# Query tiles loaded once to half of the partitions, and written to both halves by GpSimd

## The chip, the cores and the metric

The kernel runs on one core of a Trainium2 chip. The metric is the device time of one execution in microseconds. Times of before are three executions and one more under the profiler.

## What is computed

One layer of an encoder over 2048 tokens (a grid of 32 rows by 64 columns) of width 1024, in float32. Only the neighbourhood attention matters for the change; the rest is dense products around it.

```python
h = rms_norm(x, norm1_g[l])
proj = h @ w_in[l]
...
q = rms_norm(q, q_g) * jnp.asarray(hd ** -0.5, dtype=q.dtype)
k = rms_norm(k, k_g)
...
sc = jnp.einsum('bhqd,bhiqjd->bhqij', q_r, k_win).astype(jnp.float32)
sc = sc + bias[None]
p = jax.nn.softmax(sc.reshape(bsz, n_h, GRID_W, kh * WIN_COLS), axis=-1)
return jnp.einsum('bhqij,bhiqjd->bhqd', p, v_win)
...
merged = gates[..., :D_MODEL] * (y_a @ w_o_a[l]) + gates[..., D_MODEL:] * (y_b @ w_o_b[l])
x = x + merged @ w_out[l]
h2 = rms_norm(x, norm2_g[l])
x = x + jnp.square(jax.nn.relu(h2 @ w_ff1[l])) @ w_ff2[l]
```

Each query sees a window of 8 rows by 16 columns of keys; there are 8 heads of 64.

## The kernel before, in words

A float32 operand is split into a high part and a low rest (both float32r), so that three fast products replace one slow one. The stages follow one another: the projections and gates, the values and queries, the attention, the merge with the output projection, and twice the two products of the MLP. Intermediate results go through tensors in DRAM: `qs` holds the queries (64 dimensions by head of a pair, part, pair and token), `ks` the keys.

The attention goes through 16 units, 4 pairs of heads by 4 blocks of 8 grid rows. `unit` (L1152) plans the loads of one: for each of the two heads a key tile (`load_k`, L1162) and a query tile (`load_q`, L1173, and `order`, L1178), then value tiles and bias tiles. The key tile holds the keys' high parts in partitions 0 to 63 and their low rests in 64 to 127, 64 dimensions each. A product with it therefore wants the query's 64 dimensions twice, in both halves of the partitions. `load_q` gets them by two DMAs from the same place of `qs`, one to each half (L1176). `order` then makes the tile `q` from the loaded `qn` by four copies on GpSimd, one for each block of 16 columns, which reorder the tokens and round to float32r (L1181). A copy has 128 partitions and 256 elements in each.

`scores` (L1221) computes one column block: the product of q and keys on PE (L1234), on VectorE the bias and the maximum (L1248), on ScalarE the exponential (L1249), then the normalising multiply of one head on VectorE (L1256) and of the other on ScalarE (L1259). `turn` transposes the result on PE (L1279) and copies it out of PSUM (L1286, L1289); `products` multiplies it with the values (L1306). Between them stand fill products of the other branch (`branch_units`, L335), 32 in all, with inputs `y`, gates `g` and results `ma`.

The order of all instructions comes from a planner (`Plan`, L88). PE's steps are a list. Everything that prepares a step or follows one is a chain of stages, each with an engine, a cost in microseconds, the buffers that it takes and gives back, and a lead: so long before the first step that needs the chain it is issued at the latest. The planner walks along the steps with a clock for each engine, issues a stage earlier where the engine, its inputs and the buffers (51 in all) allow it, and may put a stage of ScalarE or VectorE off by a step. Nearly all transfers are issued on SP's queue. The cost of a stage only moves the planner's clocks, and so the order.

Of the kernel before, what the change touches and what calls it, by code (L numbers as in the profile page):

```python
# [24 lines left out]
HD = 64  # L25
# [249 lines left out]
class Block:  # L275
# [876 lines left out]
    def unit(self, pair, rb):  # L1152


        nc, plan = self.nc, self.plan
        r0, n, _ = ROWBLK[rb]
        rows = range(r0 // 2, (r0 + n + 1) // 2)
        ks, qs, vs = [], [], []
        for hd in range(2):
            e = {}  # L1160

            def load_k(e=e, hd=hd):  # L1162
                e[0] = self.take([n, GW], F32R, "kst")
                nc.sync.dma_start(
                    e[0][1].rearrange("p r c -> p (r c)").bitcast(F32),
                    self.ks[:, :, hd, pair, r0 * GW : (r0 + n) * GW].rearrange("l d t -> (l d) t"),
                )

            give = lambda e=e: self.give(e[0][0])
            ks.append((e, plan.chain([Stage("SP", 1.6, load_k, 1, 0, 12, 3.0)], tuple(self.k_done[t] for t in rows), hold=(1, give))))  # L1170
            e = {}

            def load_q(e=e, hd=hd):  # L1173
                e[1] = self.take([2, 512], F32, "qn")
                for dup in range(2):
                    nc.sync.dma_start(e[1][1][dup * HD : (dup + 1) * HD], self.qs[:, hd, :, pair, rb * 512 : (rb + 1) * 512])  # L1176

            def order(e=e):  # L1178
                e[0] = self.take([4, 2, P], F32R, "q")
                for cb in range(4):  # L1180
                    nc.gpsimd.tensor_copy(  # L1181
                        e[0][1][:, cb].rearrange("p l (r c) -> p (l r) c", c=16),
                        e[1][1].rearrange("p l (r f c) -> p f (l r) c", f=4, c=16)[:, cb],
                    )
                self.give(e[1][0])

            give = lambda e=e: self.give(e[0][0])
            qs.append((e, plan.chain([Stage("SP", 1.8, load_q, 1, 0, 16, 3.0), Stage("POOL", 3.0, order, 1, 1, 6, 0.3)], tuple(self.q_done[t] for t in range(4 * rb, 4 * rb + 4)), hold=(1, give))))
        for c2 in range(2):
            e = {}  # L1190

            def load_v(e=e, c2=c2):
                e[0] = self.take([2, 4, P], F32, "vw")
                for cb in range(2 * c2, 2 * c2 + 2):
                    w = COLBLK[cb][1]
                    per = P // w
                    f = n // per
                    v = e[0][1][:, cb % 2]
                    src = self.vs[cb][r0 : r0 + n, :, pair * P : (pair + 1) * P]
                    nc.sync.dma_start(v[: per * w, :f, :], src[: f * per].rearrange("(j r) k d -> (r k) j d", r=per))  # L1200
                    if n % per:
                        nc.sync.dma_start(v[: n % per * w, f, :], src[f * per :].rearrange("r k d -> (r k) d"))

            give = lambda e=e: self.give(e[0][0])
            vs.append((e, plan.chain([Stage("SP", 2.4, load_v, 1, 0, 10, 3.0)], tuple(self.v_done[t] for t in rows), hold=(1, give))))
        if rb != 2:
            kind = ROWBLK[rb][2]
            for ct in range(3):
                e = {}

                def load_b(e=e, ct=ct, kind=kind):
                    w = KIND_N[kind] * KIND_W[ct]
                    e[0] = self.take([2, w], F32, "bias")
                    src = self.tb[ct][kind][2 * pair : 2 * pair + 2].rearrange("h r c k -> (r c) h k")
                    nc.sync.dma_start(e[0][1], src)

                give = lambda e=e: self.give(e[0][0])
                self.bias[pair, ct, kind] = (e, plan.chain([Stage("SP", 1.6, load_b, 1, 0, 10, 3.0)], (self.bias_done,), hold=(1, give)))
        return ks, qs, vs

    def scores(self, pair, rb, cb, unit):  # L1221

        nc, plan = self.nc, self.plan
# [42 lines left out]
    def turn(self, rb, cb, p):  # L1266
# [25 lines left out]
        return e  # L1292

    def products(self, rb, cb, unit, pT, po, o):
        nc, plan = self.nc, self.plan
        n, w = ROWBLK[rb][1], COLBLK[cb][1]
# [121 lines left out]
    POOL, MM = 1.5, 0.2267  # L1418
# [556 lines left out]
```

## Time and profile before

| | |
|---|---|
| three executions | 2676.95, 2681.66, 2684.58 us (median 2681.66) |
| profiled execution | 2676.33 us, span 2674.6 us |
| busy in the span | PE 95%, DVE (VectorE) 68%, ACT (ScalarE) 45%, POOL (GpSimd) 45% |
| attention stage | 838 to 1117 us of the span |
| moved in the run | 569.14 MB, mean 213 GB/s |

The span is from the first to the last instruction; the profiled execution's own time holds 1.7 us more. An engine that is idle costs nothing unless the next work waits for it, so the rows on who waits for whom matter more than the busy shares.

### The profile page before, as it was taken

What the parts mean: (1) busy time and instruction counts of PE and PEld (TensorE: products, weight loads), DVE (VectorE), ACT (ScalarE), POOL (GpSimd) and SP (SyncE); (2) the same over time, 40 slices, a digit from 0 to 9 for tenths busy, and PEclk for the clock granted to TensorE, in tenths of its full rate; (3) what the DMA queues carried; (4) which work ended last, traced back from release to release, by engine and by line L of the source; (5) the groups of instructions that cost most, each with busy time, mean ns of one, the idle gap of its engine ahead of it and who ended that gap; (6) DMA issues with size and microseconds to landing.
All of it is one profiled execution on the core that took longest, in us unless ns stands there. A gap on an engine that the chain in (4) does not pass through costs nothing.

```text
span 2674.6 us, 34179 instructions
## 1 busy us (share of the span) xinstructions
PE 2533.7 (95%) x11832; PEld 2054.3 (77%) x11832; DVE 1809.7 (68%) x2492; ACT 1196.6 (45%) x1889; POOL 1206.0 (45%) x828
## 2 busy tenths in 40 slices
PE   7999999997898899899998999899999999989999
PEld 6777887875777677688887888787787888868777
DVE  5668657658677565563646555788878556688786
ACT  6556446555444555532343343543334434453331
POOL 3565554433341111142535676654344767655341
PEclk9999999998999999999999999999999999999999
DMA  6878768778679999987765443655446544465442
GB/s 202 268 242 269 226 234 285 210 223 274 175 199 270 305 325 308 335 295 244 260 228 179 152 146 142 235 173 171 138 135 216 197 149 151 146 220 192 150 146 98
DMA packets 409962, 569.14 MB, mean 213 GB/s; under 512 B 36606, under 2 KB 280382, under 8 KB 409790
## 3 DMA queue, kind: packets, MB, share of 16 engines
q1 hardware_dynamic: 405646, 566.96, 66.3%
q8 instruction: 93, 1.52, 0.2%
q10 hardware_dynamic: 4144, 0.02, 0.1%
q14 instruction: 79, 0.65, 0.1%
HBM read 363.89 MB, written 202.98 MB: 212 GB/s over the span
## 4 chain that ended last, share of the span: by engine, by line
PE 64%; DMA 11%; DVE 10%; issue 2%; SPq 2%; ACT 2%; POOL 0%; DVEq 0%; ACTq 0%; POOLq 0%
PE z L1555 26%; PE x L1555 13%; PE fg L335 12%; PE y L1555 7%; DVE r_lo L1436 2%; DVE x_r L1523 2%; DVE o L1886 2%; PE z L725 2%; PE pv L1306 1%; PE s L1234 1%; DMA x_r<-wf 1%; DMA vw<-vs 1%; DMA x_r<-xf 1%; PE x L725 1%; PE pTp L1279 1%
## 5 line engine op out<-in xcount | busy, mean ns | idle before, releaser
L1555 PE MATMUL z<-x_t,t_hi 128*128 128x512 f32 x1184 | 369.0, 393 | 23.6 <-DVE o L1886 15.1
L1478 POOL TENSOR_TENSOR w_s<-w_r 128x512 f32<-128x512 f32 (+3 forms) x87 | 153.1, 1759 | 431.5 <-PE z L1555 243.4
L1436 DVE TENSOR_TENSOR r_lo<-w_r,r_hi 128x1024 fp32r<-128x1024 f32 (+3 forms) x174 | 272.2, 1565 | 64.7 <-ACT r_hi L1432 60.3
L1555 PEld LDWEIGHTS z<-x_t,t_hi 128*128 128x128 f32 x1184 | 219.9, 188 | 81.6 <-ACT r_hi L1432 14.2
L1555 PE MATMUL z<-x_t,t_lo 128*128 128x512 f32 x592 | 231.3, 391 | 0.0
L1432 ACT CAST r_hi<-w_r 128x1024 fp32r<-128x1024 f32 (+3 forms) x174 | 171.3, 985 | 102.8 <-PE z L1555 75.6
L1555 PE MATMUL x<-x_r,t_hl 128*128 128x512 f32 x888 | 215.8, 391 | 0.2 <-DVE x_r L1523 0.2
L1555 PEld LDWEIGHTS x<-x_r,t_hl 128*128 128x128 f32 x888 | 167.0, 188 | 36.1 <-DVE x_r L1523 0.7
L1555 PE MATMUL z<-x_t,r_hi 128*128 128x512 f32 x592 | 184.2, 392 | 7.9 <-DVE o L1886 7.6
L1555 PE MATMUL z<-x_r,r_hi 128*128 128x512 f32 x592 | 186.2, 396 | 2.2 <-DVE x_r L1523 2.2
L1555 PE MATMUL y<-x_r,r_hi 128*128 128x512 f32 x592 | 182.5, 389 | 0.0
L1555 PE MATMUL x<-x_r,r_hi 128*128 128x512 f32 x592 | 182.3, 389 | 0.0
L335 PE MATMUL fg<-y,w_hi 128*128 128x512 f32 x512 | 163.2, 400 | 12.3 <-DMA y<-ya 8.0
L1523 DVE TENSOR_TENSOR x_r<-x_r,x_r 128x1024 fp32r<-128x1024 f32 x104 | 154.5, 1498 | 26.3 <-ACT x_r L1519 26.1
L1181 POOL CAST q<-qn 128x256 fp32r<-128x256 f32 x128 | 48.2, 419 | 254.3 <-DMA qn<-qs 162.1
L1479 POOL TENSOR_TENSOR w_r<-w_r,w_r 128x512 f32<-128x512 f32 (+3 forms) x87 | 152.5, 1752 | 12.4 <-issue 2.8
L335 PE MATMUL fg<-mg,w_hi 128*128 128x512 f32 x512 | 157.8, 389 | 0.0
L1484 POOL TENSOR_TENSOR w_s<-w_r 128x512 f32<-128x512 f32 (+3 forms) x87 | 154.6, 1777 | 4.2
L1519 ACT CAST x_r<-x_r 128x1024 fp32r<-128x1024 f32 x104 | 108.4, 1052 | 93.6 <-PE x L1555 29.3
L1519 ACT CAST x_t<-x_t 128x1024 fp32r<-128x1024 f32 (+1 forms) x104 | 85.0, 835 | 130.1 <-PE z L1555 110.1
L1485 POOL TENSOR_TENSOR w_s<-w_r,w_s 128x512 f32<-128x512 f32 (+3 forms) x87 | 118.4, 1360 | 46.4 <-DVE r_lo L1436 21.9
L1436 DVE TENSOR_TENSOR t_lo<-w_s,t_hi 128x1024 fp32r<-128x1024 f32 (+3 forms) x87 | 137.8, 1586 | 1.7 <-ACT t_hi L1432 1.7
(255 smaller groups left out, 6070.0 us busy)
## 6 DMA issues: line engine op xcount, KB each, us to landing
w_r<-in_w_ff_dram SPq DMA_DIRECT2D x116, 512.0 KB
x_r<-af SPq DMA_DIRECT2D x64, 512.0 KB
w_r<-in_w_in_dram SPq DMA_DIRECT2D x34, 512.0 KB
gt<-fe SPq DMA_DIRECT2D x32, 512.0 KB
x_r<-xf SPq DMA_DIRECT2D x32, 512.0 KB
qn<-qs SPq DMA_DIRECT2D x64, 256.0 KB
g<-gt SPq DMA_DIRECT2D x64, 256.0 KB
x<-x SPq DMA_DIRECT2D x32, 512.0 KB
```

Of the source, the lines that this page charges most:

```text
L335: self.nc.tensor.matmul(out, w[p], x[q], start=(i == 0 and j == 0), stop=(i == n - 1 and j == 2))
L725: nc.tensor.matmul(out, a[u], b[v], start=(p in (1, 5, 2) and k == 0 and j == 0), stop=(k == 3 and j == 2), skip_group_check=p in (6, 3, 7 ...
L1432: nc.scalar.copy(e[name + "_"][1][0], e[name][1])
L1436: nc.vector.tensor_tensor(lo, e[name][1], hi.bitcast(F32), ALU.subtract)
L1478: nc.gpsimd.tensor_tensor(s23[:, :, 1], r1[:, :, 0], r1[:, :, 1], ALU.subtract)
L1479: nc.gpsimd.tensor_tensor(r1[:, :, 1], r1[:, :, 1], r2[:, :, 1], ALU.add)
L1484: nc.gpsimd.tensor_tensor(s23[:, :, 0], r1[:, :, 1], r1[:, :, 0], ALU.subtract)
L1485: nc.gpsimd.tensor_tensor(e["t4"][1], r2[:, :, 0], s23[:, :, 0], ALU.subtract)
L1519: nc.scalar.copy(hi, lo.bitcast(F32))
L1523: nc.vector.tensor_tensor(lo, lo.bitcast(F32), hi.bitcast(F32), ALU.subtract)
L1555: nc.tensor.matmul(out, a[u], b[v], start=(p in (1, 5, 2) and k == 0 and j == 0), stop=(k == n - 1 and j == 2), skip_group_check=p in (6, ...
L1886: nc.vector.tensor_tensor(v, bank, v, ALU.add)
```

## The change

One DMA loads the query tile to partitions 0 to 63. For each column block two copies of 64 partitions on GpSimd take the place of one of 128: the first writes the lower half, the second reads the lower half of `qn` and writes the upper half of `q`. The planner's costs of the two stages become 0.9 (from 1.8) and 3.6 (from 3.0).

```diff
             def load_q(e=e, hd=hd):
                 e[1] = self.take([2, 512], F32, "qn")
-                for dup in range(2):
-                    nc.sync.dma_start(e[1][1][dup * HD : (dup + 1) * HD], self.qs[:, hd, :, pair, rb * 512 : (rb + 1) * 512])
+                nc.sync.dma_start(e[1][1][:HD], self.qs[:, hd, :, pair, rb * 512 : (rb + 1) * 512])
 
             def order(e=e):
                 e[0] = self.take([4, 2, P], F32R, "q")
                 for cb in range(4):
-                    nc.gpsimd.tensor_copy(
-                        e[0][1][:, cb].rearrange("p l (r c) -> p (l r) c", c=16),
-                        e[1][1].rearrange("p l (r f c) -> p f (l r) c", f=4, c=16)[:, cb],
-                    )
+                    for dup in range(2):
+                        nc.gpsimd.tensor_copy(
+                            e[0][1][dup * HD : (dup + 1) * HD, cb].rearrange("p l (r c) -> p (l r) c", c=16),
+                            e[1][1][:HD].rearrange("p l (r f c) -> p f (l r) c", f=4, c=16)[:, cb],
+                        )
                 self.give(e[1][0])
 
             give = lambda e=e: self.give(e[0][0])
-            qs.append((e, plan.chain([Stage("SP", 1.8, load_q, 1, 0, 16, 3.0), Stage("POOL", 3.0, order, 1, 1, 6, 0.3)], tuple(self.q_done[t] for t in range(4 * rb, 4 * rb + 4)), hold=(1, give))))
+            qs.append((e, plan.chain([Stage("SP", 0.9, load_q, 1, 0, 16, 3.0), Stage("POOL", 3.6, order, 1, 1, 6, 0.3)], tuple(self.q_done[t] for t in range(4 * rb, 4 * rb + 4)), hold=(1, give))))
```

On SP's queue, in the attention, the loads of one unit's two query tiles stand between a gate load and the value loads (qn is the loaded query tile, vw the value window, ma a fill product's result):

```order
 L1392 DMA ma<-g 128x512
 L1453 DMA g<-gt 128x512
-L1176 DMA qn<-qs 64x2x512 x4
+L1175 DMA qn<-qs 64x2x512 x2
 L1200 DMA vw<-vs_74 120x3x128
```

Four loads became two; their neighbours on the queue are the same.

On GpSimd the copies of the whole attention follow one another, after the last operation of the stage before (x_r is an input of the projections):

```order
 L701 TENSOR_TENSOR x_t_6326<-x_t_6326 128x512
 L701 TENSOR_TENSOR x_r_6291<-x_r_6291,x_r_6389 128x1024
-L1181 CAST q<-qn 128x256 x128
+L1181 CAST q<-qn 64x256 x256
 L1622 TENSOR_TENSOR g<-g 128x512 x16
```

The copies are twice as many with half the partitions, and nothing else stands between them, before or now.

On ScalarE, at a column block of 15 rows by 32 columns (p is the exponential of a block's scores, pT its transpose on the way out of PSUM):

```order
 L1432 CAST w_hi<-w 128x1024
-L1259 ACTIVATE p<-p,rec 128x480 x2
-L1289 COPY pT<-pTp 96x128
-L1286 COPY pT<-pTp 128x384
+L1259 ACTIVATE p<-p,rec 128x480
+L1289 COPY pT<-pTp 96x128
+L1286 COPY pT<-pTp 128x384
+L1259 ACTIVATE p<-p,rec 128x480
 L1249 ACTIVATE p,sums<-p,nmx 128x360 x2
```

The second of two multiplies moved behind the copies of the block before it; this pattern comes again in most units, and VectorE's order changes likewise.

## Rows read from the trace of the kernel before

**Rows 1.** The page, its span and TensorE's line of section 1

```profile
span 2674.6 us, 34179 instructions
...
PE 2533.7 (95%) x11832; PEld 2054.3 (77%) x11832; DVE 1809.7 (68%) x2492; ACT 1196.6 (45%) x1889; POOL 1206.0 (45%) x828
```

**Rows 2.** Stretches of the attention stage; the first row names the columns

```profile
core 0: us, PE busy (x) PEld busy (x) DVE busy (x) ACT busy (x) POOL busy (x), PEclk, DMA share, GB/s
838.00:1117.00 279.00, 257.98 (x1852) 200.29 (x1850) 172.06 (x551) 159.49 (x454) 43.62 (x116) 0.98 1.05 310
904.00:945.00 41.00, 33.74 (x233) 24.18 (x232) 21.50 (x71) 19.76 (x60) 6.02 (x16) 1.00 1.02 300
945.00:977.00 32.00, 31.20 (x241) 25.39 (x240) 20.95 (x68) 19.14 (x54) 5.75 (x16) 1.00 1.08 321
977.00:995.00 18.00, 15.21 (x108) 11.17 (x109) 10.01 (x35) 8.54 (x28) 3.03 (x8) 1.00 1.06 337
1045.00:1086.00 41.00, 36.05 (x241) 26.57 (x238) 21.05 (x71) 20.01 (x62) 6.18 (x16) 0.92 1.00 302
```

**Rows 3.** Waits of TensorE, 838 to 1117 us: total us, times, longest

```profile
PE fg L335 <- DMA y<-ya: 8.0, 11, 1.5
PE pv L1306 <- DMA vw<-vs: 5.1, 9, 1.0
PE s L1234 <- DMA kst<-ks: 3.5, 7, 1.2
```

**Rows 4.** Waits of VectorE in the same stretch

```profile
DVE p L1248 <- DMA bias<-tb: 9.9, 7, 2.4
```

**Rows 5.** Waits of the DMA queue's own engine in the same stretch

```profile
SPq L1164 <- DMA qn<-qs: 17.7, 25, 1.0
```

**Rows 6.** Transfers of the same stretch: all packets, issues of query loads

```profile
DMA packets 68714, 86.52 MB, mean 310 GB/s; under 512 B 5174, under 2 KB 42457, under 8 KB 68684
...
qn<-qs SPq DMA_DIRECT2D x56, 256.0 KB
```

**Rows 7.** Tile qn in the whole run: ns min/median/max, first and last start

```profile
L1181 POOL CAST q<-qn x128: 392/402/596, 801.0 to 1097.2; 128x256 fp32r<-128x256 f32 x128
L1176 SPq DMA_DIRECT2D qn<-qs x64: 573/600/1278, 794.5 to 1088.9; - x64
```

**Rows 8.** Timeline of units, engine by engine: start us, us, engine, line, what

```profile
980.84 3.46 SPq L1176 DMA_DIRECT2D qn<-qs  x4
...
1006.78 0.65 DVE L1256 TENSOR_SCALAR p<-p,rec 128x480 f32<-128x480 f32 x1
...
1006.77 1.61 POOL L1181 CAST q<-qn 128x256 fp32r<-128x256 f32 x4 [15.16 <-DMA qn<-qs]
1008.95 1.43 POOL L1181 CAST q<-qn 128x256 fp32r<-128x256 f32 x4 [0.57 <-DMA vw<-vs]
...
1013.35 0.60 PE L1234 MATMUL s<-kst,q 128*128 128x360 f32 x2
...
1079.08 1.61 POOL L1181 CAST q<-qn 128x256 fp32r<-128x256 f32 x4 [15.73 <-DMA qn<-qs]
1081.56 1.56 POOL L1181 CAST q<-qn 128x256 fp32r<-128x256 f32 x4 [0.86 <-DMA qn<-qs]
...
1085.75 0.59 PE L1234 MATMUL s<-kst,q 128*128 128x360 f32 x2
```

**Rows 9.** Groups by shape, GpSimd, whole run: busy us, mean ns | idle

```profile
L1478 POOL TENSOR_TENSOR w_s<-w_r 128x256 f32<-128x256 f32 x4 | 3.0, 742 | 6.0 <-issue 6.0
```

**Rows 10.** Groups by shape, VectorE, 838 to 1117 us

```profile
L1256 DVE TENSOR_SCALAR p<-p,rec 128x480 f32<-128x480 f32 x16 | 8.6, 535 | 0.6
...
L1256 DVE TENSOR_SCALAR p<-p,rec 128x360 f32<-128x360 f32 x16 | 6.5, 407 | 0.6
...
L1256 DVE TENSOR_SCALAR p<-p,rec 128x384 f32<-128x384 f32 x8 | 3.8, 477 | 0.3
...
L1256 DVE TENSOR_SCALAR p<-p,rec 128x264 f32<-128x264 f32 x8 | 2.9, 357 | 0.3
```

## The prediction

> **What bounds the kernel now.** I read the page first. PE is busy 95% of a span of 2674.6 us [rows 1], so a change pays only where PE waits, and this one touches only the attention stage, where the q loads and the reordering copies are. The stretches come next: from 838 us (the first product of queries and keys) to 1117 us PE is busy 257.98 of 279.00 us, so it is idle for 21.0 us, and the DMA engines are full: their share reads 1.05 [rows 2]. The idle time is lumpy. In three stretches of together 100 us it is 41.00 - 33.74 = 7.3 us, 18.00 - 15.21 = 2.8 us and 41.00 - 36.05 = 5.0 us, 15.0 of the 21.0 (with rounding); between them, from 945 to 977, PE is busy 31.20 of 32.00 us and the DMA engines are still full at 1.08 [rows 2].
>
> Who ends PE's waits is in the list of waits: inputs of the fill products (y) 8.0 us, values 5.1 us, keys 3.5 us, all three DMA landings, 16.6 us in sum [rows 3]. The other 4.4 of the 21.0 us are left for ScalarE and VectorE. VectorE, which feeds PE, itself waits 9.9 us for bias tiles [rows 4]. So this stage is bound by transfers at places where much is loaded at once, and by PE nearly everywhere else.
>
> The queue's own waits show how one load holds another: key loads wait 17.7 us, 25 times, for landings of q loads, though no key load needs q's data [rows 5]. I read it so that SP's queue has only so many transfers in flight; a q load then costs its bytes and a place in the queue.
>
> **What the change removes.** Each q tile is fetched once instead of twice: 64 q loads become 32 [rows 7]. In the stage 56 of them are issued, 256.0 KB each, so 28 go: 28 x 256 KiB = 7.3 MB of 86.52 MB, 8.5% [rows 6]. The places in the queue fall alike. If every transfer takes its share of a full queue, the stage's transfers would take 279 x (1 - 0.085) = 255 us. That is below what PE works, 258 us, so PE becomes the bound and not all of the 24 us can be had. SP also issues 32 fewer at a median of 600 ns [rows 7]; SP's issuing is not what PE waits for, so I count nothing for that.
>
> **What comes back.** In the three lumps, 100 us of full transfers shrink by 8.5 us, against 15.0 us of idle. The other 179 us hold 6.0 us of idle; I take 2 us, since the 4.4 us of ScalarE and VectorE stay wherever they are. Between the lumps SP gets ahead by up to 8.5% too and carries some of it into the next lump, as far as the 51 buffers let it; I take 3 of the 6.5 us that are left there. Sum 13.5 us. Bounds: 0 (all waits form again) and 21.0 us (no idle left), to which the far end adds the clock: from 1045 to 1086 the granted clock reads 0.92 against 1.00 in the other stretches shown [rows 2], so 0.08 x 41 = 3.3 us of that stretch may be matmuls stretched at the lower level, 24 us in all.
>
> **What it adds on GpSimd.** 128 copies [rows 7] become 256, of 64 partitions with the same 256 elements in each. A run of four takes 1.43 to 1.61 us [rows 8], from 0.36 us apiece. Half of the new ones read partitions 0 to 63 and write 64 to 127, which no row shows. Bounds: 0.18 us (time goes by the number of partitions) and 0.74 us, the two-input operation on as many elements [rows 9]. I take 0.36 us, because the nearest row is the same copy. The busy time then grows by 128 x 0.36 = 46 us over the run; GpSimd has the room, since it is busy 43.62 of the stage's 279 us [rows 2], and does nothing but these copies there.
>
> What counts is when the second tile of a unit is ready. In two units the copies end at 1008.95 + 1.43 = 1010.38 and 1081.56 + 1.56 = 1083.12 us, and the product that reads them starts at 1013.35 and 1085.75 us, so 3.0 and 2.6 us are left [rows 8]. From the first copy to the last it takes 3.6 and 4.0 us now; sixteen in a row would take 16 x 0.36 = 5.8 us, 2.0 us more than their mean. The first tile lands earlier by about one load's share: four issues take 3.46 us [rows 8], so 0.8 us. The last copy then ends 1.2 us later, inside the 2.6 us. I count 0 for that, and 1 us in all for the odd unit that misses.
>
> **A second price** is on VectorE. Its normalising multiply takes 357 and 407 ns at 264 and 360 elements, 0.52 ns per element, so 420 and 469 ns are due at 384 and 480; the means there are 477 and 535 ns [rows 10]. One of 0.65 us starts at 1006.78, with copies from 1006.77 [rows 8]: the larger forms meet the copies. The excess is 8 x 57 + 16 x 66 = 1.5 us in the stage. Twice the copies make it some 3 us; of the 1.5 us more I put 0.5 us on PE's path, bounds 0 and 1.5.
> [...]
>
> **Edits that only reorder.** The planner's costs of the two steps change, so ScalarE now runs one tile's copies before the next tile's multiply, and VectorE's order shifts likewise; PE's order is the same. It moves waits that are 4.4 us today: 0, with bounds of 4 us either way. On SP all other transfers keep their order but for one key load.
>
> **The sum.** 13.5 - 1 - 0.5 = 12 us. The profiled execution took 2676.3 us, so it would take 2664.3. It is the fastest of the four executions shown; the median of the three others is 2681.66 and the mean of all four 2679.9 us. I set the forecast from that mean: **2668 us**.
>
> **Rivals.**
> - *The waits form again* (0.22). The plan issues loads a fixed lead ahead, so with less traffic they may land as late before PE as now, the lumps being bursts of y, bias and keys that still arrive together. For it: PE's waits stand in lumps, not everywhere. Against it: the engines are full between the lumps too. It gains 3 us at most: 2677 to 2681 us, counted from the mean and with the two prices.
> - *Relief on the wrong half* (0.07). What goes is the load that wrote partitions 64 to 127; partitions 0 to 63 receive as many q bytes as before. If the two halves have limits of their own, every load to 128 partitions still ends with the lower half, nothing is gained and the prices of 1.5 us stay: 2681 us from the mean. No row parts the two halves; that the stage keeps all engines full speaks mildly against it.
> [...]
> - *Copies come last* (0.09, slower). Place: the second tile of a unit. Price: sixteen copies. The point: with d from one copy to the next the last ends 16d - 3.8 - 0.8 later than now, and that exceeds the mean of 2.8 us left at d = 0.46 us. At 0.74 us it is 11.8 - 4.6 - 2.8 = 4.4 us in each of the 14 units after the first two (whose queries come long before), 62 us, less the 12 of relief: 2680 + 50 = 2730 us. For it: a copy to other partitions has no row. Against it: the plain copy stands at 0.36.
>
> **Chances.** Forecast 0.62, rivals 0.22, 0.07, 0.09. A difference under 0.3% (8 us) is about what a measurement of this kernel cannot tell from none. The forecast's own range is 2655 to 2675 us, a gain of some 5 to 25 us; 0.03 of its 0.62 stays within 0.3%. Faster 0.60, same 0.30 (that 0.03 and most of the first two rivals), slower 0.10. The range takes in the first two rivals, 2655 to 2683 us, and leaves out the slow one and a few ends.
>
> **What the profile after would show.** Right: the stage from the first to the last score product shorter by about 10 us, its bytes down by 7 MB, PE's waits for y, values and keys down from 16.6 to about 6 us, 256 copies at 0.36 us, no PE wait for q. Wrong: the DMA share still above 1.0 with the same waits (the first two rivals), or PE waiting for GpSimd's copies (the third).

## The result and the profile after

The changed kernel takes 2653.32 us (median of 7 executions), the kernel before in the same comparison 2680.94 us; the ratio is 0.9911, 95% interval 0.9898 to 0.9925. That is 24 us faster by the ratio, where the forecast was 12; the two medians lie 27.6 us apart. The median lies 1.7 us under the lower end of the range, 2655 us; the ratio applied to the level from which the forecast was counted, 0.9911 x 2679.9 = 2656.0 us, lies just inside.

The page of the changed kernel, its span and the engines' line, against [rows 1]: the span is 22.7 us shorter, GpSimd is busy 61 us longer.

```profile
span 2651.9 us, 34278 instructions
...
PE 2525.9 (95%) x11832; PEld 2052.2 (77%) x11832; DVE 1811.7 (68%) x2492; ACT 1196.1 (45%) x1889; POOL 1266.7 (48%) x956
```

From the first to the last product of queries and keys the kernel before takes 838.3 to 1116.4 us, the changed one 839.2 to 1093.0 us. The whole gain is made there: it begins 0.9 us later, and from its end to the end of the span it is 1558.2 us before and 1558.9 us now. First the kernel before, then the changed one with four of its stretches (columns as in [rows 2]):

```profile
838.30:1116.40 278.10, 257.08 (x1844) 199.56 (x1843) 171.46 (x547) 158.59 (x453) 43.32 (x115) 0.98 1.05 310
```

```profile
839.20:1093.00 253.80, 249.45 (x1844) 197.68 (x1843) 170.13 (x547) 157.87 (x453) 97.63 (x235) 1.00 1.05 313
904.00:920.00 16.00, 14.52 (x108) 10.59 (x106) 9.54 (x34) 8.64 (x30) 6.38 (x16) 1.00 0.94 282
920.00:945.00 25.00, 24.73 (x181) 19.15 (x181) 15.73 (x49) 14.97 (x42) 8.57 (x22) 1.00 1.07 302
945.00:977.00 32.00, 31.94 (x243) 25.83 (x242) 21.40 (x73) 19.27 (x59) 13.06 (x33) 1.00 1.07 339
1045.00:1060.00 15.00, 15.00 (x112) 11.79 (x110) 10.41 (x34) 9.02 (x28) 4.42 (x11) 1.00 1.07 299
```

278.1 us became 253.8, 24.3 us less. A second profile of the changed kernel (a0, beside e10 below) has a stage of 251.2 us, so a difference of 2 or 3 us between two profiled stages tells little. PE's idle time fell from 278.10 - 257.08 = 21.0 to 253.80 - 249.45 = 4.4 us, and its busy time by another 7.6 us. The DMA share is 1.05 as before. The lump that stood from 904 to 945 us with 7.3 us of idle [rows 2] is down to 1.5 + 0.3 us, and the stretch at 1045 us, where the clock read 0.92, shows 1.00 up to 1060.

Who ends the waits of PE's matmuls in the changed kernel, and below it the wait for q, which only PE's weight loads (PEld) show:

```profile
PE pTp L1279 <- ACT p L1259: 1.3, 3, 0.9
PE pv L1306 <- DMA vw<-vs: 0.7, 2, 0.3
PE fg L335 <- DMA y<-ya: 0.6, 1, 0.6
...
PE s L1234 <- DMA kst<-ks: 0.3, 1, 0.3
```

```profile
PEld s L1234 <- POOL q L1181: 1.3, 5, 0.6
```

The three transfers that ended 16.6 us of waits [rows 3] now end 0.7 + 0.6 + 0.3 = 1.6 us. A new wait is there: PE's weight loads wait for the copies of q 5 times, 1.3 us; no matmul is listed as waiting for them. The stage's transfers, against [rows 6]:

```profile
DMA packets 64781, 79.37 MB, mean 313 GB/s; under 512 B 4732, under 2 KB 41952, under 8 KB 64750
...
qn<-qs SPq DMA_DIRECT2D x28, 256.0 KB
```

What a unit's copies look like now (one unit of sixteen copies, and a weight load of PE that waits for copies), and VectorE's multiply beside them:

```profile
992.40 7.35 POOL L1181 CAST q<-qn 64x256 fp32r<-64x256 f32 x16 [10.56 <-DMA qn<-qs]
```

```profile
998.85 0.63 PEld L1234 LDWEIGHTS s<-kst,q 128*128 128x128 f32 x4 [0.17 <-POOL q L1181]
```

```profile
L1256 DVE TENSOR_SCALAR p<-p,rec 128x480 f32<-128x480 f32 x16 | 8.6, 540 | 0.6
...
L1256 DVE TENSOR_SCALAR p<-p,rec 128x384 f32<-128x384 f32 x8 | 3.6, 456 | 0.3
```

Sixteen copies take 7.35 us, 0.46 us each, where [rows 8] had 1.43 to 1.61 us for four. The multiply did not get slower by more copies: 540 and 456 ns against 535 and 477 [rows 10].

### The profile page after: what moved, and what is told of

Same layout as the page of the kernel before. It is cut to its first block, busy times and chain, and to the rows that moved or that the text cites. A ratio compares the mean times of both kernels' runs of the same rounds, so it can differ in the third digit from the quotient of the medians.

```text
span 2651.9 us, 34278 instructions
## 1 busy us (share of the span) xinstructions
PE 2525.9 (95%) x11832; PEld 2052.2 (77%) x11832; DVE 1811.7 (68%) x2492; ACT 1196.1 (45%) x1889; POOL 1266.7 (48%) x956
## 4 chain that ended last, share of the span: by engine, by line
PE 62%; DVE 13%; DMA 9%; issue 3%; ACT 2%; SPq 2%; POOL 0%; DVEq 0%; ACTq 0%
PE z L1555 26%; PE x L1555 13%; PE fg L335 11%; PE y L1555 7%; DVE x_r L1523 2%; DVE r_lo L1436 2%; DVE o L1886 1%; PE z L725 1%; DMA tb<-tbi 1%; PE s L1234 1%; PE pv L1306 1%; DMA g<-gt 1%; DVE t_lo L1436 1%; PE x L725 1%; PE pTp L1279 1%
## 5 line engine op out<-in xcount | busy, mean ns | idle before, releaser
L1181 POOL CAST q<-qn 64x256 fp32r<-64x256 f32 x256 | 106.9, 418 | 173.9 <-DMA qn<-qs 152.7
```

What stands on the lines that cost most here:

```text
L1181: nc.gpsimd.tensor_copy(e[0][1][dup * HD : (dup + 1) * HD, cb].rearrange("p l (r c) -> p (l r) c", c=16), e[1][1][:HD].rearrange("p l (r f ...
```

## The experiments

The theory after the result: in this stage the time goes with the bytes that the DMA engines move, down to what PE needs. Its rivals: places in SP's queue and SP's time to issue, the new order on ScalarE and VectorE, and limits of each half of the partitions. Ratios are to the kernel before on the same chip, with 95% intervals; "the stage" is from the first to the last product of queries and keys.

### e1: the second load back

```diff
-                nc.sync.dma_start(e[1][1][:HD], self.qs[:, hd, :, pair, rb * 512 : (rb + 1) * 512])
+                for dup in range(2):
+                    nc.sync.dma_start(e[1][1][dup * HD : (dup + 1) * HD], self.qs[:, hd, :, pair, rb * 512 : (rb + 1) * 512])
```

> The changed kernel with its second load put back: both halves of the partitions are loaded again, the 256 copies of 64 partitions and the order on every engine stay. Bytes theory (the stage is bound by what the DMA engines move): the stage is back at 277 to 279 us from the first to the last score product, the ratio to the kernel before is 0.997 to 1.003, PE's waits for y, values and keys are back at 14 us or more. Order theory (the gain came with the new order of ScalarE and VectorE and the copies): the stage stays at 254 to 258 us and the ratio at 0.990 to 0.993.

Measured: 1.0003 (0.9988 to 1.0019), no different from the kernel before. The stage and PE's waits in it:

```profile
840.50:1115.30 274.80, 256.25 (x1844) 198.13 (x1843) 171.24 (x547) 158.19 (x453) 96.75 (x233) 0.99 1.06 315
```

```profile
PE fg L335 <- DMA y<-ya: 6.5, 11, 2.0
PE pv L1307 <- DMA vw<-vs: 6.0, 9, 1.3
...
PE s L1235 <- DMA kst<-ks: 1.0, 2, 0.5
```

The stage is back at 274.8 us and the three waits at 13.5 us, a little under the 277 us and the 14 us that were expected at least. So the load is the whole of the gain that the times show, and the 256 copies cost nothing that can be measured, though they keep GpSimd busy for 97 us of the stage. PE's busy time is back too (256.25 us) with the same products in the same order: it goes with the waits.

### e2: as many loads, half of the bytes

```diff
-                nc.sync.dma_start(e[1][1][:HD], self.qs[:, hd, :, pair, rb * 512 : (rb + 1) * 512])
+                for l in range(2):
+                    nc.sync.dma_start(e[1][1][:HD, l], self.qs[:, hd, l, pair, rb * 512 : (rb + 1) * 512])
```

> The changed kernel with its one load of 256 KB cut in two of 128 KB (high parts, low rests): as many loads as before the change, half of the bytes. Bytes theory: the stage stays within 3 us of the changed kernel's 254 us, ratio to the kernel before 0.989 to 0.994. Places theory (a load costs its place in SP's queue and SP's time to issue it, not its bytes): the stage is back near 275 us, ratio 0.997 to 1.003; in between, both take part in that share.

Measured: 0.9917 (0.9898 to 0.9936). The stage and its q loads:

```profile
842.20:1095.30 253.10, 249.03 (x1844) 197.92 (x1843) 169.76 (x547) 157.86 (x453) 95.53 (x232) 1.00 1.04 313
```

```profile
qn<-qs SPq DMA_DIRECT2D x56, 128.0 KB
...
SPq L1164 <- DMA qn<-qs: 4.8, 15, 0.6
```

56 loads stand in the stage as before the change, of 128 KB, and it takes 253.1 us. The last line is the wait of [rows 5]. A place in the queue and SP's issue cost nothing that the times show; the bytes do.

### e4: the planner's costs alone

```diff
-Stage("SP", 1.8, load_q, 1, 0, 16, 3.0), Stage("POOL", 3.0, order, 1, 1, 6, 0.3)
+Stage("SP", 0.9, load_q, 1, 0, 16, 3.0), Stage("POOL", 3.6, order, 1, 1, 6, 0.3)
```

> The kernel before with nothing but the planner's two new costs (0.9 and 3.6): two loads, 128 copies of 128 partitions, but the new order on ScalarE and VectorE. My forecast's term for the order is 0 us: ratio 0.998 to 1.002, stage 276 to 280 us. Order theory: 5 us or more of the 24 us come from it, stage 273 us or less, ratio 0.998 or less.

Measured: 0.9991 (0.9977 to 1.0005). The stage took 275.4 us, 0.6 us under the expected lower end, at 316 GB/s:

```profile
838.30:1113.70 275.40, 256.88 (x1844) 201.15 (x1843) 171.05 (x547) 158.66 (x453) 44.38 (x116) 0.98 1.06 316
```

```profile
PE pv L1306 <- DMA vw<-vs: 7.7, 8, 1.8
PE fg L335 <- DMA y<-ya: 6.7, 9, 1.6
PE s L1234 <- DMA kst<-ks: 1.6, 3, 0.7
```

The transfers end 16.0 us of waits, about as before. The stage is 2.7 us shorter than that of the kernel before, about as much as two profiles of the changed kernel differ, and the times show nothing for the new order.

### e5: half of the q loads left out

The second head's scores are computed with the first head's queries; the planner also orders VectorE, ScalarE and the loads otherwise.

```diff
             def load_q(e=e, hd=hd):
-                e[1] = self.take([2, 512], F32, "qn")
+                if hd:
+                    return
+                e[1] = qn[0] = self.take([2, 512], F32, "qn")
...
-            def order(e=e):
+            def order(e=e, hd=hd):
+                e[1] = qn[0]
                 e[0] = self.take([4, 2, P], F32R, "q")
```

> The changed kernel with half of its q loads left out: the second head of each pair copies the first head's queries, so the second heads' scores are those of other queries. 4.2 MB less again. PE-bound theory (the bytes no longer limit; PE works 250.65 of 255 us): at most 4 us more, stage 250 to 254 us, ratio 0.988 to 0.992. Bytes theory carried on (the DMA share still reads 1.05, so bytes still limit): half of the change's gain again, stage 240 to 244 us, ratio 0.986 or less.

Measured: 0.9883 (0.9863 to 0.9904), the stage 250.2 us:

```profile
840.10:1090.30 250.20, 247.50 (x1844) 198.46 (x1843) 169.97 (x547) 158.41 (x453) 90.17 (x224) 1.00 0.99 309
```

PE is idle for 2.7 us, the DMA share of the whole stage falls below 1 for the first time, and of the 12 us that bytes alone would give only 3.6 come, or 1.0 against the second profile of the changed kernel. So in the changed kernel the bytes no longer set the stage's time alone, and PE, busy 247.5 of 250.2 us here, is close to its limit. A share of 1.05 said nothing about that, since it stood in both kernels.

### e8 and e9: the bytes of before, to one half or to both

Both have a second load of the same queries that nobody reads, into a buffer of its own: e8 to partitions 0 to 63, e9 to 64 to 127 (there the slice is `[(i - 1) * HD : i * HD]`).

```diff
+                e[2] = self.take([2, 512], F32, "qx")
-                nc.sync.dma_start(e[1][1][:HD], self.qs[:, hd, :, pair, rb * 512 : (rb + 1) * 512])
+                for i in (1, 2):
+                    nc.sync.dma_start(e[i][1][:HD], self.qs[:, hd, :, pair, rb * 512 : (rb + 1) * 512])
```

> The changed kernel with a second load of the same queries, which nobody reads, to partitions 0 to 63 of a buffer of its own: the bytes of before, all in the lower half. Compared with e9_own_upper, where that load goes to partitions 64 to 127. Rival of the halves (each half of the partitions has a limit of its own): slower than e9 by 8 us or more, stage 285 us or more. Bytes theory (the transfers share one limit): the same as e9 within 4 us, and like the kernel before, ratio 0.996 to 1.004, stage 275 to 280 us.

> As e8_both_lower, with the second load in partitions 64 to 127 of the buffer of its own. Bytes theory: like the kernel before, ratio 0.996 to 1.004, stage 275 to 280 us, the same as e8. Rival of the halves: faster than e8 by 8 us or more.

Measured: e8 1.0067 (1.0043 to 1.0090), e9 1.0014 (1.0001 to 1.0026). The stage of e8 with PE's longest wait, then that of e9:

```profile
840.00:1136.60 296.60, 265.75 (x1844) 206.67 (x1843) 171.34 (x547) 158.76 (x453) 99.24 (x240) 0.94 1.06 295
```

```profile
PE pv L1308 <- DMA vw<-vs: 15.7, 9, 4.7
```

```profile
838.10:1116.80 278.70, 259.41 (x1844) 200.83 (x1843) 171.14 (x547) 157.74 (x453) 97.07 (x236) 0.97 1.06 312
```

With the same order and the same bytes e8 is 15 us slower (2694.36 against 2678.94 us): it moves 295 GB/s in the stage against 312, and the value loads keep PE waiting 15.7 us. The bytes theory had e8 like e9, and there it fell: bytes to one half cost more than bytes to both. e9, even, is like the kernel before in its stage, 278.7 us. The 18 us between the two stages are more than the 15 us of the times: e8's profiled run, 2702.32 us, is the slowest of its five, and its granted clock in the stage reads 0.94 against 0.97.

### e6: the copies in another order

```diff
                 for cb in range(4):
                     for dup in range(2):
...
+                for dup in range(2):
+                    for cb in range(4):
                         nc.gpsimd.tensor_copy(
```

> The changed kernel with its two loops of copies exchanged: first four copies within partitions 0 to 63, then four from there to 64 to 127. It shows the spacing of each kind by itself. If writing to other partitions sets the 0.44 us from one copy to the next: the first four stand at 0.35 us as the copies of 128 partitions did, the last four at 0.44 or more. If 64 partitions set it: all at 0.44 us. Time as the changed kernel, ratio 0.989 to 0.993, either way.

Measured: 0.9927 (0.9906 to 0.9949), with the changed kernel inside the interval. GpSimd's timeline, one unit in each row:

```profile
907.75 5.99 POOL L1181 CAST q<-qn 64x256 fp32r<-64x256 f32 x16 [13.41 <-DMA qn<-qs]
...
938.73 6.07 POOL L1181 CAST q<-qn 64x256 fp32r<-64x256 f32 x16 [7.13 <-DMA qn<-qs]
```

Sixteen copies take 5.99 to 6.07 us and no longer 7.35. Taken from the single starts in the trace, the median from one copy to the next is 0.346 us among the copies that read and write the lower half, 0.346 us among those that read the lower and write the upper half, and 0.44 us from the last of the first kind to the first of the second. In the changed kernel, where the two kinds alternate, it is 0.44 to 0.46 us all through. So both of the expected reasons fell: neither 64 partitions nor the way to other partitions costs anything, but a change of the half written does, some 0.1 us each time. Before the change each copy wrote both halves, and none changed.

### e7: more lead

```diff
-Stage("SP", 0.9, load_q, 1, 0, 16, 3.0), Stage("POOL", 3.6, order, 1, 1, 6, 0.3)
+Stage("SP", 0.9, load_q, 1, 0, 20, 3.0), Stage("POOL", 3.6, order, 1, 1, 10, 0.3)
```

> The changed kernel with 4 us more lead for the q loads and copies (20 and 10 us): it can only remove PE's 1.3 us of waits for q and what follows from them. Expected 0 to 3 us faster than the changed kernel, ratio 0.988 to 0.992, PE's waits for q at 0.3 us or less; if the earlier loads push others back instead, y, values and keys end more of PE's waits than the 1.6 us of the changed kernel, and the ratio is 0.992 or more.

Measured: 0.9940 (0.9921 to 0.9959), no gain over the changed kernel. PE's waits:

```profile
PE pv L1306 <- DMA vw<-vs: 1.8, 2, 1.0
PE fg L335 <- DMA y<-ya: 1.8, 2, 0.9
```

```profile
PEld s L1234 <- POOL q L1181: 0.3, 2, 0.2
```

PE's weight loads wait 0.3 us for q, and PE 1.8 + 1.8 us for y and values in place of 0.6 + 0.7. That is the second of the two expected outcomes, what is loaded earlier pushes other loads back, as far as one profile can show it: the interval overlaps that of the changed kernel.

### e10: even halves, and the changed kernel beside it

To e6 is added that the second head's tile goes to the upper half, and is copied from there:

```diff
-                nc.sync.dma_start(e[1][1][:HD], self.qs[:, hd, :, pair, rb * 512 : (rb + 1) * 512])
+                nc.sync.dma_start(e[1][1][hd * HD : (hd + 1) * HD], self.qs[:, hd, :, pair, rb * 512 : (rb + 1) * 512])
...
-                            e[1][1][:HD].rearrange("p l (r f c) -> p f (l r) c", f=4, c=16)[:, cb],
+                            e[1][1][hd * HD : (hd + 1) * HD].rearrange("p l (r f c) -> p f (l r) c", f=4, c=16)[:, cb],
```

> The changed kernel with its loops of copies exchanged as in e6, and the tiles of the pair's second head loaded to partitions 64 to 127 in place of 0 to 63, so that the two halves receive equal bytes. If the uneven halves still cost the changed kernel something, as the 15 us between e8 and e9 would let one think: faster than the changed kernel by 3 us or more, ratio 0.990 or less, stage 250 us or less. If PE is the bound: within 3 us of it, ratio 0.989 to 0.993, stage 250 to 254 us.

> The changed kernel itself, beside e10 on the same chip: ratio 0.989 to 0.993, stage 252 to 256 us.

Measured: e10 0.9884 (0.9866 to 0.9902), the changed kernel beside it 0.9900 (0.9882 to 0.9917); medians 2648.38 and 2654.36 us. The two stages, e10 first:

```profile
838.00:1087.80 249.80, 247.54 (x1844) 198.65 (x1843) 170.88 (x547) 157.82 (x453) 85.56 (x232) 0.99 1.05 321
```

```profile
845.10:1096.30 251.20, 248.77 (x1844) 198.88 (x1843) 169.35 (x547) 157.75 (x453) 91.80 (x227) 0.99 1.05 311
```

e10 is the fastest kernel of this study that computes the layer (e5, at 2648.03 us, does not), 33 us under the kernel before by its median. In the stage it moves 321 GB/s against 311 and takes 249.8 against 251.2 us; the list of waits names no transfer and no copy for its matmuls, nor does that of the changed kernel beside it. By its numbers e10 falls under the first expectation, uneven halves that still cost something. But the intervals of the two overlap, so that e10 beats the changed kernel by its 6 us is likely and not shown. The other order of the copies, which e10 has too, gave nothing by itself in e6. The stage of the changed kernel was expected at 252 to 256 us and took 251.2.

## Why the prediction was right, and where it was off by half

**What bounds the stage**: right. Transfers set it; e1 gives the time back with the load alone. **Places in the queue**: wrong as a cost. e2 has as many loads as the kernel before, and neither its time nor its stage shows a cost of places; the waits of key loads for q's landings [rows 5] fall to 4.8 us there, from 17.7.

**What comes back** is the term that failed: 13.5 us, measured 24.3. I argued that transfers take 255 us without the second load, that this "is below what PE works, 258 us, so PE becomes the bound and not all of the 24 us can be had". The transfers' part of this was right: the stage came out at 253.8 us. The 258 us were no floor. PE's busy time fell to 249.45 us with the waits, and came back to 256.25 in e1. The far bound had put 3.3 us of it down to the clock from 1045 to 1086 us, and e1 speaks against that: its clock reads 1.00 in that stretch and from 845 us to the end of the stage, and its PE is busy only 0.8 us less than in the kernel before. Two stretches of e1:

```profile
845.00:1115.30 270.30, 251.75 (x1831) 194.36 (x1830) 168.89 (x540) 154.29 (x445) 93.18 (x224) 1.00 1.06 315
1045.00:1086.00 41.00, 35.72 (x256) 26.29 (x255) 23.65 (x79) 21.28 (x65) 12.87 (x32) 1.00 1.05 319
```

The single matmuls in the traces show where the busy time went. One that follows another without a gap overlaps with it and adds 0.13 us to the busy time; one that starts behind a gap adds its whole length, 0.40 us in the mean before the change. Behind a gap stand 43 of the stage's matmuls before, 20 in the changed kernel and 48 in e1. What they add over 0.13 us each comes to 11.3, 4.2 and 11.3 us, so 7.1 of the 7.6 us went with these (an estimate, since the profile models the ends of matmuls). Each wait thus cost its idle time and some busy time behind it.

The second half of the failure is the split into lumps. I let relief between the lumps count for 3 of 6.5 us; the stage's gain is about its whole share of bytes, so what is saved anywhere seems to put SP ahead for the next lump, with buffers enough. No run shows this apart. Sum of the measured parts: idle time 16.6 us less (transfers 15.0 of it) and busy time 7.6 us less.

That the range held is in part luck. The gain of 24 us is the far end of the sum's bounds, which I reached by adding the clock to all of the idle time; the clock is not what gave it, and by its median the changed kernel lies outside.

**Copies on GpSimd**: 0.46 us and not 0.36, so 7.35 us for sixteen against 5.8, and 61 us more on GpSimd over the run against 46. It used up the slack that I had reckoned as left over: PE's weight loads wait 1.3 us for q, and 0.5 us in the second profile, where I put 1 us. The point at which the slow rival decides, 0.46 us, was met, and just about nothing happened, as it should at that point. e1 bounds the whole cost of the copies by its interval, 5 us. **VectorE's multiply**: 0.5 us put, none found. Twice the copies did not double the excess: counted in the traces, copies met 23 of the stage's 64 multiplies before and 27 after, and these took 1.9 and 1.7 us more in sum than undisturbed ones of their size. **Order**: 0, and e4 agrees.

**The rivals.** The waits did not form again. Copies did not come last by more than 1.3 us. Relief on the wrong half gave a premise that the runs support and the wrong outcome: a second load cost 15 us more to the half that the first goes to than to the other (e8, e9), and still the relief of the upper half alone brought the full share of the bytes. An estimate shows how both can hold. Take it that all of a stage's bytes but those of the q loads go evenly to the two halves (28 q loads are 7.34 MB). Then the lower half moved 86.24 / 2 MB in 278.1 us before, 155 GB/s; (79.37 - 7.34) / 2 + 7.34 MB in 253.8 us in the changed kernel, 171 GB/s; and (87.41 - 14.68) / 2 + 14.68 MB in 296.6 us in e8, 172 GB/s. So before the change the lower half was below a rate that it reached later, and relief of the upper half could count whole; the changed kernel may stand close to a limit of the lower half as well as to PE's. The even e10, at 321 GB/s in all, fits this and does not prove it; no run tests it alone. The transfers of the stage before and in e8:

```profile
DMA packets 68548, 86.24 MB, mean 310 GB/s; under 512 B 5156, under 2 KB 42411, under 8 KB 68518
...
DMA packets 69773, 87.41 MB, mean 295 GB/s; under 512 B 5269, under 2 KB 43349, under 8 KB 69742
```

**The signs.** The mark of a wrong prediction was "the DMA share still above 1.0 with the same waits". The share stayed at 1.05 while the waits went, so the share as a sign tells nothing and the waits do. Of the marks of a right one the bytes came as named (6.9 MB less), the stage's gain and the waits went further (24.3 us for 10, and 1.6 us for 6), and the copies took 0.46 us for 0.36. The mark of the third rival, PE waiting for copies, was there too, but only for 1.3 us of its weight loads.

## What to carry to other kernels

Where the DMA engines are full through a whole stage and PE's waits end with landings, reckon with the stage's time times the share of bytes removed (here 279 x 0.085 = 24 us, and 24.3 us came), and take PE's busy time in that stage as no floor: it holds time that comes with the waits (7.6 us here), and only a kernel without them shows what is left. With 1.6 us left of PE's waits for transfers, fewer bytes brought little more: half of the q loads left out shortened the stage by 3.6 us, or 1.0 against the second profile (e5). A second copy of a tile in SBUF can be made by an idle engine in place of a second load; make the copies of one half together (6.0 us for sixteen in place of 7.35), and let the loads fill both halves of the partitions evenly (15 us between e8 and e9; the 6 us of e10 are not shown).

## What the runs showed of the hardware that was not expected

- From copy to copy on GpSimd it is 0.346 us within a run that writes one half of the partitions, whether it reads the same half or the other, and 0.44 to 0.46 us where writes change between the halves (e6 against the changed kernel).
- The same 8.4 MB more into partitions 0 to 63 cost 15 us more than into 64 to 127, where the first load goes to 0 to 63 already (e8, e9), at 295 against 312 GB/s.
- A DMA share of 1.05 stood with 16.6 us of PE's waits for transfers, and with 1.6 us.
- A matmul that started behind a gap put 0.40 us on PE's busy time where one in a run put 0.13 us, and PE's busy time in the same stage fell by 7.6 us when the waits went, 7.1 of them with these by the estimate above.
